# Order of the output projection, of the residual loads, and of the last chunked heads in a two-layer mixer kernel

## The chip, the cores and the metric

The kernel runs on one core of one Trainium2 chip. The metric is the device time of one execution in microseconds (us). Three runs of the kernel before gave 1920.71, 1923.3 and 1924.99 us, so its median is 1923.3 us. Times "at 382.7" are microseconds from the start of the profiled execution's span.

## What is computed

Two layers (`DEPTH` = 2) over 512 rows of 1024 values in float32. Each layer multiplies its input with a wide matrix `w_in`, runs three attention branches on the slices, gates and sums them, and projects the sum with `w_out`; a residual and a normalisation follow, then a feed-forward block (FFN) with its own residual and normalisation.

```python
h = jnp.einsum('bsd,de->bse', x, w_in[l])
rq, rk, rv, rg, cq, ck, cv, dq, dk, dv, gates = jnp.split(h, splits, axis=-1)
o_a = _retention(...)          # 4 heads
o_b = _chunk_attention(...)    # 8 heads
o_c = _diff_attention(...)     # 4 heads, two score matrices each
g = jax.nn.sigmoid(gates + b_merge[l]).reshape(B, S, N_BRANCHES, D)
merged = (g[:, :, 0] * (o_a @ w_branch_a[l]) + g[:, :, 1] * (o_b @ w_branch_b[l])
          + g[:, :, 2] * (o_c @ w_branch_c[l]))
mix = jnp.einsum('bsd,de->bse', merged, w_out[l])
x = _layer_norm(DEEPNORM_ALPHA * x + mix, ln1_g[l], ln1_b[l])
u_gate, u_up = jnp.split(jnp.einsum('bsd,df->bsf', x, w_ffn_in[l]), 2, axis=-1)
ffn = jnp.einsum('bsf,fd->bsd', jax.nn.silu(u_gate) * u_up, w_ffn_out[l])
x = _layer_norm(DEEPNORM_ALPHA * x + ffn, ln2_g[l], ln2_b[l])
```

## The kernel before

Every float32 operand is split into a high and a low part (`xTh`, `xTl`; `wh`, `wl`), and a product is three matmuls (`mm3`, lines 122 to 124). The high part is a cast on ACT, the low part a subtraction on DVE that needs the cast. The program is a list of *items*. An item names its weights and a function with two products, j = 0 and j = 1; between the two, and behind the second, small *groups* of other work are called (`between`). Weights are fetched up to three items ahead: the DMA into a staging tile `st` (4 of them), the cast to `wh` on ACT and the subtraction to `wl` on DVE (3 of each).

**What sets the order on the engines.** The code is traced once and a scheduler lays it out: each engine runs its queue strictly in the laid order and waits at the head of it. The scheduler takes work by program order where it is ready by its own estimate. One rule of it matters here: almost all tiles come from one pool `g` of 61 slots, and all matmul outputs from one pool of 8 PSUM banks, and in each pool the instructions that write a tile for the first time are laid out in program order, over all engines. A first writer that is late holds back the first writers of all tiles that the code makes after it. A bank goes to the next tile when the tile that had it has been read for the last time.

**The last chunked heads.** For head h, `s_c1(h)` makes four score products (`psc`, 4 banks) and the softmax (DVE line 437, ACT line 439), `s_c2(h)` transposes them (`ptr`, 10 transposes, 3 banks) and splits them into `cPh` and `cPl` (line 106, 112), and `s_c3(h)` multiplies with the values (`pco`, 1 bank; the copy `cos` on ACT, line 941, then the sum `cot` on DVE, line 942, which frees the bank). `u_dqk(h)` projects the queries and keys of differential head h (`pt`, 24 matmuls each) and rotates them: four copies `sw` on ACT, three DVE operations that make `rot`, and casts to `qs` or `ks` on ACT. `s_d0(0, 0)` makes the first score products of the differential heads, `v_back(dv)` reloads eight value tiles, `u_gate(1, i)` computes gates.

```python
(u_dqk(0), *c(7)), (u_gate(1, 0), *c(8)), (u_dqk(1), [v_back(dv)], [s_c3(7)] + d(0)[1]), (u_branch(1, 0), *d(1)),
```

`c(7)` stands for the groups `[s_c3(5), s_c1(7)]` and `[s_c2(6)]`, `c(8)` for `[s_c3(6)]` and `[s_c2(7)]`; `d(0)[1]` is `[s_d0(0, 0)]`.

**Branch C and the merge.** `u_branch(2, i)` multiplies the differential output (`oc`, made by `s_d4`) with `w_branch_c` into columns i and i + 4, multiplies with the gate (line 1083), adds to the sum of the other branches (`acc`, line 1087) and splits the result: `m` (of i) and `m2` (of i + 4). `s_mleft(k)` and `s_mright(k)` make the differences `sa` and `sb` of columns k and k + 4 and split them into `s12` and `s43`.

**The output projection** is a scheme of seven products in place of eight (`Chain`): `m1`, `m2`, `y`, `x`, `v`, `g`, `h`, 24 matmuls each. `m1` uses `m`, `m2` and `h` use `m2`, `y` and `x` use `s12`, `v` and `g` use `s43`. Its weights are sums of quarters of `w_out`: one staging tile is loaded for `m1`, and after the split for `m1` a DMA on the POOL queue adds the next quarter to it (line 178) for `y`, then in the same way for `x`, then for `h`. `m2` and `v` have plain loads, `g` a tile of its own (`c`). The results are added to the residual rows `z` (8 tiles; `load_res`, lines 459 and 1175 to 1178), whose last addition is followed by the statistics and, in the item with `whole`, by the normalisation; `bc` are four tiles of the norm's factors (line 465). `s_turned(0)` transposes the normalised rows 0 to 255 (`px`) for the FFN.

Of the kernel before, what the change touches and what calls it, by code (L numbers as in the profile page):

```python
# [15 lines left out]
ALU = mybir.AluOpType  # L16

P = 128
S = 512
D = 1024  # L20
NT = S // P
# [35 lines left out]
def trunk(ctx, tc, x_in, xT_in, w_in, ret_norm_g, da_norm_g, lq1, lk1, lq2, lk2, w_a, w_b, w_c, b_merge, w_out,  # L57
# [558 lines left out]
    def layer(l):  # L616
# [253 lines left out]
        def v_back(dst):  # L870
            def fn():
                for k, away in list(dst.items()):
                    dst[k] = g(F32R, "vhl")
                    nc.sync.dma_start(f(dst[k]), away)
            return fn
# [48 lines left out]
        def s_c3(h):  # L924
            def fn():
                p, j = divmod(h, 2)
                if j == 0:
                    ob[p] = g(name="cot")
                o_ = ob[p]
                pT = cP.pop(h)  # L930
                ps = bank("pco")
                for mt in range(NT):
                    b, o = PACK[mt]
                    w = S - P * mt
                    vt, c = v_of(cv, mt, h, 64)
                    hi = (ps[:, P * mt:], vt[:, c:c + P], pT[b].hi[:, o:o + w])
                    lo = (ps[:64, P * mt:], vt[:, c:c + 64], pT[b].lo[:, o:o + w])
                    for x in ((hi, lo) if mt == 0 else (lo, hi)):
                        nc.tensor.matmul(*x, start=mt == 0 and x is hi, stop=mt == NT - 1 and x is hi)
                t = g(name="cos")  # L940
                nc.scalar.copy(t[:64], ps[64:128])
                nc.vector.tensor_add(o_[64 * j:64 * j + 64], ps[:64], t[:64])
                if j:
                    ob[p] = Pair("ob")
                    split(ob[p], o_)
            return fn
# [5 lines left out]
        def u_dqk(h):  # L952
            def fn(wt):
                if "cd" not in tabs:
                    tabs["cd"], tabs["sd"], tabs["mask"] = g(name="cosd"), g(name="sind"), g(name="mask")
                    nc.sync.dma_start(tabs["cd"], rope_da[0])
                    nc.sync.dma_start(tabs["sd"], rope_da[1])
                    nc.vector.memset(tabs["mask"], 0.0)
                    nc.vector.memset(tabs["mask"][0:64, 0:64], -NEG)
                dqk[h] = QK()  # L960
                dqk[h].set_q(rotary(proj_T(xT, wt, 0), tabs["cd"], tabs["sd"], 32), -DA_DH ** -0.5)
                between()
                dqk[h].set_k(rotary(proj_T(xT, wt, P), tabs["cd"], tabs["sd"], 32))
            return [([wcols(DQ + P * h, P), wcols(DK + P * h, P)], KT)], fn
# [99 lines left out]
        def u_gate(br, i):  # L1064
            def fn(wt):
                for j, d in enumerate(tiles(br, i)):
                    gate_done(br, d, proj_T(xT, wt, P * j), (br, i) in EARLY)
                    between()
            return [(cols_of(W, GATE + D * br, br, i), KT)], fn
# [31 lines left out]
        def s_mleft(k):  # L1101
            def fn():
                mq[k].left(acc[k], acc[k + 4], 0.5)
            return fn
# [6 lines left out]
        def c(i):  # L1111

            return ([st(h) for st, h in ((s_c3, i - 2), (s_c1, i)) if 0 <= h < CA_HEADS],
                    [s_c2(i - 1)] if 0 <= i - 1 < CA_HEADS else [])

        def d(i):
# [6 lines left out]
                mid = [s_d3(h - 1)] if h >= 1 else []  # L1123
            return mid, [s_d0(h, j)]

        def u_rvg(hp):
            return u_two(Close(W, 0, 4, (RV + 512 * hp, RG + 512 * hp)), xq,
                         functools.partial(rv_done, hp), functools.partial(rg_done, hp))
# [11 lines left out]
        for (specs, fn), *groups in start + [  # L1140
            (w["x"], [p["a"]]), (u_gate(0, 3),), (w["g"],), (w["h"], [p["c"]]),
            (p["m1"], [s_dh(0)]), (p["y"], [], [s_r1(0)]), (p["v"], [s_dh(1)]), (p["m2"], [], [s_r1(1)]),
            (p["x"], [q["a"]]), (u_rqk(rq, RQ, 1),), (p["g"], [q["c"]]), (p["h"],),
            (q["m1"], [], [s_r2(0)]), (q["y"], [s_r2(1)]), (u_rqk(rk, RK, 1), [], [s_r3(0)]),
            (q["v"], [s_dh(2)], [s_r3(1)]), (q["m2"], [], [s_r1(2)]), (q["x"], [s_dh(3)]), (u_cqk(0), [], [s_r1(3)]), (q["g"],), (q["h"],),
            (u_gate(2, 0), [s_r2(2)], [s_r2(3), s_r3(2)]), (u_cqk(1), [s_r3(3)] + c(0)[0], c(0)[1]),
            (u_branch(0, 0), c(1)[0] + [v_back(cv)], c(1)[1]), (u_branch(0, 1), *c(2)), (u_cqk(2), *c(3)),
            (u_branch(0, 2), *c(4)), (u_cqk(3), *c(5)), (u_branch(0, 3), *c(6)), 
            (u_dqk(0), *c(7)), (u_gate(1, 0), *c(8)), (u_dqk(1), [v_back(dv)], [s_c3(7)] + d(0)[1]), (u_branch(1, 0), *d(1)),
            (u_gate(1, 1), [], d(2)[0] + d(2)[1]), (u_branch(1, 1), *d(3)), (u_dqk(2),),  # L1150
            (u_gate(1, 2), *d(4)), (u_branch(1, 2), *d(5)), (u_dqk(3),),
            (u_gate(1, 3), *d(6)), (u_branch(1, 3), *d(7)), (u_gate(2, 1), [s_d4(2)], [s_d2(3)]),
            (u_gate(2, 2), [s_d3(3)], [s_d4(3)]),
            (u_branch(2, 0), [], [s_mleft(0)]), (u_branch(2, 1), [], [s_mleft(1)]), (u_gate(2, 3), [s_mright(0)], [s_mright(1)]),
            (u_branch(2, 2), [], [s_mleft(2)]), (u_branch(2, 3), [], [s_mleft(3)]),
        ]:
            item(specs, fn, *groups)


        x1 = {}  # L1160
        x1T = [None] * KT
        x1f, x1q = {}, {}

        def load_res(x, src):
            x["z"] = [[g(name="z") for _ in range(2)] for _ in range(NT)]
            x["fresh"] = {(t, hf) for t in range(NT) for hf in range(2)}
            for t in range(NT):
                load_rows(x["z"][t], src[P * t:P * t + P])

        def plus(x, t, hf, ps, op, final=False):  # L1170

            z = x["z"][t][hf]
            if (t, hf) in x["fresh"]:
                x["fresh"].remove((t, hf))
                nc.vector.scalar_tensor_tensor(z, z, ALPHA, ps, op0=ALU.mult, op1=op)
            else:
                nc.vector.tensor_tensor(z, z, ps, op=op)  # L1177
            if final:
                x["n"].stats(t, hf)

        def out_items():

            hv = Chain(w_out[l], 0, 4)
            w = {}

            def it(name, i, hf, op, last=False, whole=False):
                def fn(wt):
                    if name == "m1":
                        load_res(x1, x_in if l == 0 else saved[2 * l - 1])
                        x1["n"] = Norm(x1["z"], v["g1"], v["b1"], bcast_rows(ln1_g[l:l + 1]), bcast_rows(ln1_b[l:l + 1]),  # L1190
                                       x1T, saved[2 * l], x1f)
                    on = {"x": "m1", "g": "m1", "h": "m1", "v": "y"}.get(name, name)
                    for j in range(2):
                        t = 2 * i + j
                        w[on, j] = product(mq, name, j, wt, w.pop((on, j), None))
                        plus(x1, t, hf, w[on, j], op, last)
                        if name in ("m2", "v", "h"):
                            w.pop((on, j))
                        if whole:
                            x1["n"].normalise(t)  # L1200
                        between()
                return [getattr(hv, name)], fn

            add, sub = ALU.add, ALU.subtract
            return {"c": hv.ahead_c, "m1": it("m1", 0, 0, add), "m2": it("m2", 0, 0, add, True), "y": it("y", 1, 1, add),
                    "x": it("x", 0, 1, sub), "v": it("v", 0, 1, add, True, True), "g": it("g", 1, 1, sub, True),
                    "h": it("h", 1, 0, add, True, True)}

        def s_turned(hf):
            def fn():  # L1210
                for b in range(4):
                    x1["n"].transposes_of(hf, b)
                if hf == 0:
                    x1q.update({i: Quarters(x1T[i], x1T[i + 4]) for i in range(4)})
            return fn

        o = out_items()
        for (specs, fn), *groups in [
            (o["m1"], [s_mright(2)], [o["c"]]), (o["m2"], [s_mright(3)]), (o["y"],), (o["x"],), (o["v"],),
            (o["g"], [], [s_turned(0)]), (o["h"],),  # L1220
        ]:
            item(specs, fn, *groups)

        hid = [None] * FT

# [233 lines left out]
```

## Time and profile before

| quantity | value |
|---|---|
| median of 3 runs | 1923.3 us |
| profiled execution, its own time | 1925.2 us |
| its span | 1923.4 us |
| ACT and DVE busy | 990.2 and 1391.6 us |
| mean granted clock of TensorE | 0.99 |

The profile's page has one row per engine with its busy time and a row of clock tenths. A view of waits lists, for one engine, who waited for whom (engine, line and tile of the waiting instruction, then of the releaser; total, times, longest). A view of windows has one row for a stretch A:B: its length, then for each engine the busy time and the number of instructions, the granted clock of TensorE, the share of the DMA engines and GB/s. A timeline has start, duration, engine, line, operation, output <- inputs, shapes, count, and in brackets the idle time before it with its releaser.

### The profile page before, as it was taken

To read this page: it belongs to the slowest core of one execution; us is meant where nothing else is said; L and a number is where in the kernel's file an instruction comes from. 1 tells how busy PE (TensorE), PEld (TensorE's weight loads), DVE (VectorE), ACT (ScalarE), POOL (GpSimd) and SP (SyncE) were. 2 spreads that over 40 slices of the span, in tenths; PEclk is the share of its full clock that TensorE was granted. 3 is DMA by queue.
4 is the path that set the end of the run, shared out by engine and by line. 5 is a ranking of instruction groups with operands and counts; after the bars stand their busy time and mean duration, and the time that the engine had idled before them with its cause. 6 is when DMAs were issued, how large, how long until landed. Compare 5 with 4: busy or idle time off the path is not lost. (4 is left out here: it accounts for less than half of the span.)

```text
span 1923.4 us, 23342 instructions
## 1 busy us (share of the span) xinstructions
PE 1874.9 (97%) x8754; PEld 1553.5 (81%) x8754; DVE 1391.6 (72%) x2117; ACT 990.2 (51%) x1593; POOL 132.6 (7%) x153
## 2 busy tenths in 40 slices
PE   9999999899998999999999999998999989999998
PEld 7788888778876788888878888887788768888886
DVE  6777756757677777789586768566675777778886
ACT  5555645656643544555264555456565445455541
POOL 2000000000001000010020000000000010000100
PEclk9999999999999999999999999999999999999999
DMA  9584453232267666788476844532322765777871
GB/s 289 170 269 132 121 170 116 87 99 66 82 176 175 158 175 186 181 231 197 147 221 192 247 110 142 179 90 83 110 66 72 210 161 160 184 188 206 210 197 44
DMA packets 235938, 302.89 MB, mean 157 GB/s; under 512 B 8757, under 2 KB 127633, under 8 KB 235825
## 3 DMA queue, kind: packets, MB, share of 16 engines
q1 hardware_dynamic: 205488, 242.25, 38.7%
q0 software_dynamic: 30336, 59.15, 17.7%
q8 instruction: 69, 1.13, 0.2%
q14 instruction: 45, 0.36, 0.1%
HBM read 279.29 MB, written 22.07 MB: 157 GB/s over the span
## 5 line engine op out<-in xcount | busy, mean ns | idle before, releaser
L272 DVE TENSOR_TENSOR wl<-st,wh 128x2048 fp32r<-128x2048 f32 x140 | 320.3, 2290 | 134.9 <-ACT wh L271 134.2
L271 ACT CAST wh<-st 128x2048 fp32r<-128x2048 f32 x140 | 267.3, 1914 | 249.6 <-PE pf L124 115.5
L122 PE MATMUL pt<-xTh,wh 128*128 128x512 f32 x960 | 378.7, 395 | 2.2 <-ACT wh L154 1.8
L124 PE MATMUL pt<-xTh,wl 128*128 128x512 f32 x960 | 375.3, 391 | 0.0
L123 PE MATMUL pt<-xTl,wh 128*128 128x512 f32 x960 | 375.2, 391 | 0.0
L155 DVE TENSOR_TENSOR wl<-st,wh 128x1024 fp32r<-128x1024 f32 (+1 forms) x188 | 200.8, 1085 | 69.1 <-ACT wh L154 46.8
L154 ACT CAST wh<-st 128x1024 fp32r<-128x1024 f32 (+1 forms) x188 | 173.5, 944 | 118.4 <-PE pt L123 44.5
L122 PEld LDWEIGHTS pt<-xTh,wh 128*128 128x128 f32 x960 | 181.4, 189 | 40.6 <-ACT wh L154 2.9
L124 PEld LDWEIGHTS pt<-xTh,wl 128*128 128x128 f32 x960 | 180.9, 188 | 38.2
L123 PEld LDWEIGHTS pt<-xTl,wh 128*128 128x128 f32 x960 | 181.0, 189 | 36.8 <-DVE xTl L112 0.2
L122 PE MATMUL pf<-wh,xTh 128*128 128x512 f32 x336 | 133.6, 398 | 2.3 <-ACT rph L106 0.9
L123 PE MATMUL pf<-wl,xTh 128*128 128x512 f32 x336 | 131.1, 390 | 0.0
L124 PE MATMUL pf<-wh,xTl 128*128 128x512 f32 x336 | 130.3, 392 | 0.0
L122 PE MATMUL pf<-wh,s43h 128*128 128x512 f32 x256 | 101.3, 396 | 6.4 <-ACT s43h L108 6.4
L122 PE MATMUL pf<-wh,s12h 128*128 128x512 f32 x256 | 101.5, 397 | 3.2 <-ACT wh L271 3.2
L123 PE MATMUL pf<-wl,s12h 128*128 128x512 f32 x256 | 101.0, 395 | 3.6 <-DVE wl L272 3.6
L123 PE MATMUL pf<-wl,s43h 128*128 128x512 f32 x256 | 100.9, 394 | 0.0
L124 PE MATMUL pf<-wh,s12l 128*128 128x512 f32 x256 | 100.7, 394 | 0.0
L124 PE MATMUL pf<-wh,s43l 128*128 128x512 f32 x256 | 100.3, 393 | 0.0
L746 ACT COPY tc<-pf 128x512 f32<-128x512 f32 x84 | 48.5, 590 | 81.2 <-PE pf L124 76.0
L122 PEld LDWEIGHTS pf<-wh,xTh 128*128 128x128 f32 x336 | 63.1, 188 | 19.8 <-ACT xTh L106 2.3
L124 PEld LDWEIGHTS pf<-wh,xTl 128*128 128x128 f32 x336 | 62.5, 188 | 15.3 <-DVE xTl L112 2.7
(327 smaller groups left out, 3681.5 us busy)
## 6 DMA issues: line engine op xcount, KB each, us to landing
st<-in_w_in SPq DMA_DIRECT2D x53, 1024.0 KB, 6.3
st<-in_w_ffn_in SPq DMA_DIRECT2D x38, 1024.0 KB, 5.9
st<-in_w_in SPq DMA_DIRECT2D x48, 512.0 KB, 5.2
st<-in_w_ffn_in POOLq DMA_DIRECT2D x20, 1024.0 KB, 10.8
st<-in_w_ffn_out SPq DMA_DIRECT2D x20, 1024.0 KB, 7.9
st<-in_w_ffn_out POOLq DMA_DIRECT2D x16, 1024.0 KB, 9.0
st<-in_w_in POOLq DMA_DIRECT2D x12, 1024.0 KB, 11.1
st<-in_w_ffn_in SPq DMA_DIRECT2D x24, 512.0 KB, 5.5
```

Source lines behind the costliest of these rows:

```text
L122: nc.tensor.matmul(ps, lh, rh, start=start, stop=False, skip_group_check=onto)
L123: nc.tensor.matmul(ps, lh, rl, start=False, stop=False, skip_group_check=onto)
L124: nc.tensor.matmul(ps, ll, rh, start=False, stop=stop, skip_group_check=onto)
L154: return [nc.scalar.copy(self.hi[:, a:b], self.st[:, a:b]), nc.vector.tensor_sub(self.lo[:, a:b], self.st[:, a:b], f(self.hi[:, a:b]))]
L155: nc.vector.tensor_sub(self.lo[:, a:b], self.st[:, a:b], f(self.hi[:, a:b]))]
L271: nc.scalar.copy(self.hi, st)
L272: nc.vector.tensor_sub(self.lo, st, f(self.hi))
L746: nc.scalar.copy(t[to, j], ps)
```

## The change

In both layers:

1. The output projection runs `m1, m2, y, v, x, g, h`. `x` now closes its rows (statistics and normalisation), no longer `v`.
2. The eight residual loads and the construction of the norm leave the function of `m1` and become the group `rows_in`, behind the second product of `u_gate(2, 2)` and ahead of `s_d4(3)`. The four loads of the norm's factors become the group `norm_rows` in `x`.
3. `s_mleft(2)` moves from behind `u_branch(2, 2)` to behind `u_branch(2, 3)`, ahead of `s_mleft(3)`. The load and the addition for `g` (`o["c"]`) move from `m1` to the first group of `u_branch(2, 2)`.
4. `s_c2(6)` moves from behind the key projection of `u_dqk(0)` to the group between its two projections, ahead of `s_c1(7)`.
5. `s_c3(7)` and `s_d0(0, 0)` move from behind the key projection of `u_dqk(1)` to the group between its two projections, behind `v_back(dv)`.

The other lines of the diff only move the functions ahead of their first use.

```diff
+        def rows_in():
+            load_res(x1, x_in if l == 0 else saved[2 * l - 1])
+            x1["n"] = Norm(x1["z"], v["g1"], v["b1"], None, None, x1T, saved[2 * l], x1f)
+
+        def norm_rows():
+            x1["n"].gam, x1["n"].bet = bcast_rows(ln1_g[l:l + 1]), bcast_rows(ln1_b[l:l + 1])
...
-                    if name == "m1":
-                        load_res(x1, x_in if l == 0 else saved[2 * l - 1])
-                        x1["n"] = Norm(x1["z"], v["g1"], v["b1"], bcast_rows(ln1_g[l:l + 1]), bcast_rows(ln1_b[l:l + 1]),
-                                       x1T, saved[2 * l], x1f)
...
-                    "x": it("x", 0, 1, sub), "v": it("v", 0, 1, add, True, True), "g": it("g", 1, 1, sub, True),
+                    "x": it("x", 0, 1, sub, True, True), "v": it("v", 0, 1, add), "g": it("g", 1, 1, sub, True),
...
-            (u_dqk(0), *c(7)), (u_gate(1, 0), *c(8)), (u_dqk(1), [v_back(dv)], [s_c3(7)] + d(0)[1]), (u_branch(1, 0), *d(1)),
+            (u_dqk(0), [s_c3(5), s_c2(6), s_c1(7)]), (u_gate(1, 0), [s_c3(6)], [s_c2(7)]),
+            (u_dqk(1), [v_back(dv), s_c3(7)] + d(0)[1]), (u_branch(1, 0), *d(1)),
...
-            (u_gate(2, 2), [s_d3(3)], [s_d4(3)]),
+            (u_gate(2, 2), [s_d3(3)], [rows_in, s_d4(3)]),
...
-            (u_branch(2, 2), [], [s_mleft(2)]), (u_branch(2, 3), [], [s_mleft(3)]),
+            (u_branch(2, 2), [o["c"]]), (u_branch(2, 3), [], [s_mleft(2), s_mleft(3)]),
...
-            (o["m1"], [s_mright(2)], [o["c"]]), (o["m2"], [s_mright(3)]), (o["y"],), (o["x"],), (o["v"],),
+            (o["m1"], [s_mright(2)]), (o["m2"], [s_mright(3)]), (o["y"],), (o["v"],), (o["x"], [norm_rows]),
             (o["g"], [], [s_turned(0)]), (o["h"],),
```

More of the change, by code (lines that the diff above doesn't have):

```diff
@@ L1124, in d, with load_res, plus @@
             return mid, [s_d0(h, j)]
+        x1 = {}
+        x1T = [None] * KT
+        x1f, x1q = {}, {}
+        def load_res(x, src):
+            x["z"] = [[g(name="z") for _ in range(2)] for _ in range(NT)]
+            x["fresh"] = {(t, hf) for t in range(NT) for hf in range(2)}
+            for t in range(NT):
+                load_rows(x["z"][t], src[P * t:P * t + P])
+        def plus(x, t, hf, ps, op, final=False):
+            z = x["z"][t][hf]
+            if (t, hf) in x["fresh"]:
+                x["fresh"].remove((t, hf))
+                nc.vector.scalar_tensor_tensor(z, z, ALPHA, ps, op0=ALU.mult, op1=op)
+            else:
+                nc.vector.tensor_tensor(z, z, ps, op=op)
+            if final:
+                x["n"].stats(t, hf)
@@ new lines, in rows_in, with out_items, it, fn @@
+        def rows_in():
[3 more added lines that the diff above has]
+            x1["n"].gam, x1["n"].bet = bcast_rows(ln1_g[l:l + 1]), bcast_rows(ln1_b[l:l + 1])
+        def out_items():
+            hv = Chain(w_out[l], 0, 4)
+            w = {}
+            def it(name, i, hf, op, last=False, whole=False):
+                def fn(wt):
+                    on = {"x": "m1", "g": "m1", "h": "m1", "v": "y"}.get(name, name)
+                    for j in range(2):
+                        t = 2 * i + j
+                        w[on, j] = product(mq, name, j, wt, w.pop((on, j), None))
+                        plus(x1, t, hf, w[on, j], op, last)
+                        if name in ("m2", "v", "h"):
+                            w.pop((on, j))
+                        if whole:
+                            x1["n"].normalise(t)
+                        between()
+                return [getattr(hv, name)], fn
+            add, sub = ALU.add, ALU.subtract
+            return {"c": hv.ahead_c, "m1": it("m1", 0, 0, add), "m2": it("m2", 0, 0, add, True), "y": it("y", 1, 1, add),
+                    "x": it("x", 0, 1, sub, True, True), "v": it("v", 0, 1, add), "g": it("g", 1, 1, sub, True),
+                    "h": it("h", 1, 0, add, True, True)}
@@ L1126, in u_rvg, with s_turned, fn @@
+        def s_turned(hf):
+            def fn():
+                for b in range(4):
+                    x1["n"].transposes_of(hf, b)
+                if hf == 0:
+                    x1q.update({i: Quarters(x1T[i], x1T[i + 4]) for i in range(4)})
+            return fn
+        o = out_items()
         def u_rvg(hp):
@@ L1152, in layer @@
             (u_gate(1, 3), *d(6)), (u_branch(1, 3), *d(7)), (u_gate(2, 1), [s_d4(2)], [s_d2(3)]),
-            (u_gate(2, 2), [s_d3(3)], [s_d4(3)]),
+            (u_gate(2, 2), [s_d3(3)], [rows_in, s_d4(3)]),
             (u_branch(2, 0), [], [s_mleft(0)]), (u_branch(2, 1), [], [s_mleft(1)]), (u_gate(2, 3), [s_mright(0)], [s_mright(1)]),
-            (u_branch(2, 2), [], [s_mleft(2)]), (u_branch(2, 3), [], [s_mleft(3)]),
[L1156 to L1187, printed above, removed]
-                    if name == "m1":
-                        load_res(x1, x_in if l == 0 else saved[2 * l - 1])
-                        x1["n"] = Norm(x1["z"], v["g1"], v["b1"], bcast_rows(ln1_g[l:l + 1]), bcast_rows(ln1_b[l:l + 1]),
-                                       x1T, saved[2 * l], x1f)
[L1192 to L1205, printed above, removed]
-                    "x": it("x", 0, 1, sub), "v": it("v", 0, 1, add, True, True), "g": it("g", 1, 1, sub, True),
-                    "h": it("h", 1, 0, add, True, True)}
@@ L1209, in s_turned @@
[L1209 to L1218, printed above, removed]
-            (o["m1"], [s_mright(2)], [o["c"]]), (o["m2"], [s_mright(3)]), (o["y"],), (o["x"],), (o["v"],),
+            (u_branch(2, 2), [o["c"]]), (u_branch(2, 3), [], [s_mleft(2), s_mleft(3)]),
```

## The prediction, on record before the result

> **What bounds the kernel now.** I read the page first, then the waits of PE, then windows around the two places that the diff touches, then the timelines of the engines there. The page says which engine is full:
>
> ```profile
> PE 1874.9 (97%) x8754; PEld 1553.5 (81%) x8754; DVE 1391.6 (72%) x2117; ACT 990.2 (51%) x1593; POOL 132.6 (7%) x153
> ```
>
> The change adds and removes no matmul, so it can only win back time in which PE stands still or runs at a reduced clock. The waits of PE name the places:
>
> ```profile
> PE pco L939 <- ACT cPh L106: 9.5, 2, 4.8
> PE pf L122 <- ACT s43h L108: 6.4, 2, 4.8
> PE psc L422 <- DVE cot L942: 5.4, 2, 2.7
> PE pf L122 <- ACT m L108: 3.8, 2, 1.9
> PE pf L123 <- DVE wl L272: 3.6, 2, 1.8
> PE pf L122 <- ACT wh L271: 3.2, 2, 2.3
> ```
>
> Each happens twice, once per layer, and all six lie in the code that the diff reorders: the first and third in the last chunked heads, the others in the output projection. What all of it costs is read from one window per stage and layer:
>
> ```profile
> 357.20:430.40 73.20, 65.29 (x291) 52.93 (x290) 43.01 (x87) 40.09 (x80) 1.04 (x2) 0.93 0.31 94
> 568.10:615.80 47.70, 38.37 (x146) 30.07 (x145) 31.79 (x44) 14.50 (x12) 3.68 (x4) 0.89 0.76 205
> 1315.20:1386.40 71.20, 63.44 (x287) 51.31 (x285) 43.00 (x87) 39.71 (x79) 1.04 (x2) 0.95 0.31 96
> 1524.50:1569.60 45.10, 36.37 (x146) 28.27 (x144) 31.55 (x45) 15.47 (x13) 3.06 (x3) 0.92 0.79 216
> ```
>
> Loss is the length less PE's busy time, plus the length times what the granted clock lacks to 1. Heads, layer 0: 73.20 − 65.29 = 7.91 idle and 0.07 × 73.2 = 5.1 of clock, 13.0 in all; layer 1: 7.76 + 3.56 = 11.3. Projection, layer 0: 9.33 + 5.25 = 14.6; layer 1: 8.73 + 3.61 = 12.3. The sum, **51.2 us**, bounds the gain: 1874 would be the floor.
>
> **The heads (points 4 and 5).** Why PE stood still:
>
> ```profile
> 365.24 0.44 PE L122 MATMUL pt<-xTh,wh 128*128 128x512 f32 x1
> 370.77 1.25 PE L452 MATMUL ptr<-ident,cE 128*128 128x128 f32 x10
> 382.72 0.80 PE L939 MATMUL pco<-cPh,vhl 128*128 128x512 f32 x1 [4.76 <-ACT cPh L106]
> 414.42 0.44 PE L422 MATMUL psc<-ks,qs 128*128 128x384 f32 x1 [2.69 <-DVE cot L942]
> ```
>
> ```profile
> 367.39 1.29 ACT L108 ACTIVATE qs<-rot 64x512 fp32r<-64x512 f32 x2 [2.08 <-DVE rot L391]
> 368.71 0.58 ACT L941 COPY cos<-pco 64x512 f32<-64x512 f32 x1
> 379.51 2.54 ACT L106 CAST ks<-rot 64x512 fp32r<-64x512 f32 x4 [1.98 <-DVE rot L391]
> 382.08 1.07 ACT L106 CAST cPh<-ptr 128x512 fp32r<-128x512 f32 x2
> ```
>
> The transposes of head 6 are done at 372.02, yet `cPh` is cast at 382.08, right behind the key casts. In the code `s_c2(6)` stands behind the key projection, so its first writers stand behind `ks` in pool order, and ACT waits 1.98 us for the rotation. With `s_c2(6)` ahead of the keys, `cPh` follows its transposes by a few us, long before PE reaches `s_c3(6)` at 378: the 4.76 goes.
>
> What is late next is a PSUM bank. Between the projections now stand, in order, `pco(5)`, three `ptr`, four `psc`, and then the key projection. With the query `pt` that is nine banks, the keys' is the tenth; two must have come free. The query's comes free early. The second is `pco(5)`'s, freed by `cot`:
>
> ```profile
> 369.50 0.68 DVE L942 TENSOR_TENSOR cot<-pco,cos 64x512 f32<-64x512 f32 x1
> 413.68 0.68 DVE L942 TENSOR_TENSOR cot<-pco,cos 64x512 f32<-64x512 f32 x1 [0.44 <-ACT cos L941]
> ```
>
> `cot` ends at 370.18, because `cos` (368.71) stands behind the `qs` casts, which wait for the rotation. Before, PE filled this time with the key projection (from 365.24). Now the transposes run in it, and it runs dry 1.25 us later than 365.24, at 366.5: **a new wait of 3.7**. Bounds: 0 if a bank comes free earlier; 5.6 if it is the first `ptr`, which is split on ACT behind `cos` and then on DVE, by my estimate at 372.1 (`cot`'s end, a cast of 1.07, a subtraction of some 0.7). I take 3.7, since that bank's own row shows the end.
>
> `s_c3(7)` and `s_d0(0, 0)` ahead of the keys of `u_dqk(1)`: the 2.69 is the same pattern (`cot` at 413.68 behind the key rotation), and it goes. Bounds: 0 to 2.7 of it stays, since the value reloads stand ahead of `cos(7)` in pool order:
>
> ```profile
> 397.37 8.78 SPq L874 DMA_DIRECT2D vhl<-v  x8
> ```
>
> They are issued by 406.2. PE reached the stall at 411.73; without the key product (24 matmuls of 0.23, 5.5) it has done `s_c3(7)` at 406.2 as well, so `cos(7)` hardly waits; I take 0. The keys of head 1 are rotated later by about the 3 us that the inserted work takes, and PE has work of `s_d0(0, 1)` and the gates beside it: 1.0 for a wait of the next transposes, bounds 0 and 3. Half clock: the rows of before show what a stall does to the clock.
>
> ```profile
> 1372.00:1375.40 3.40, 3.31 (x10) 2.42 (x9) 3.05 (x11) 2.31 (x9) 0.00 (x0) 0.50 0.02 5
> ```
>
> This window stands behind the layer-1 copy of the 2.69 stall: 3.4 us at half clock, 1.7 lost. So I put 1.7 behind the new 3.7, bounds 0 and 3.4.
>
> (The Trainium skill, page "TensorE: Matmul & The Clock Gate", section "What's actually happening", gives the half rate only after a whole idle window of about 3.4 us. This row speaks against that, since 2.69 was enough, and the measurement decides. By the rule the stalls forecast below 3.4 us would cost no clock, and the time would be an estimated 3.4 us less than mine.)
>
> New loss 3.7 + 1.0 + 1.7 = 6.4 per layer, so the heads gain 13.0 − 6.4 = **6.6** and 11.3 − 6.4 = **4.9**.
>
> **The projection (points 1 to 3).**
>
> ```profile
> 570.29 1.90 ACT L271 CAST wh<-st 128x2048 fp32r<-128x2048 f32 x1 [4.85 <-DMA st<-in_w_out]
> 572.63 0.40 ACT L108 ACTIVATE m<-th 128x256 fp32r<-128x256 f32 x1
> 587.30 5.52 ACT L271 CAST wh<-st 128x2048 fp32r<-128x2048 f32 x3 [8.65 <-DMA st<-in_w_out]
> 602.10 1.90 ACT L271 CAST wh<-st 128x2048 fp32r<-128x2048 f32 x1 [6.43 <-DMA st<-in_w_out]
> 603.91 0.63 ACT L108 ACTIVATE s43h<-sb 128x512 fp32r<-128x512 f32 x1
> 1557.60 1.91 ACT L271 CAST wh<-st 128x2048 fp32r<-128x2048 f32 x1 [5.62 <-DMA st<-in_w_out]
> ```
>
> ```profile
> 589.25 2.29 DVE L272 TENSOR_TENSOR wl<-st,wh 128x2048 fp32r<-128x2048 f32 x1 [6.99 <-ACT wh L271]
> 594.25 0.42 DVE L304 TENSOR_TENSOR sb<-th,sa 128x256 f32<-128x256 f32 x1
> ```
>
> ```profile
> 561.78 1.28 POOL L178 DMA_DIRECT2D st<-in_w_out  x1 [11.03 <-DVE wl L272]
> 591.83 1.28 POOL L178 DMA_DIRECT2D st<-in_w_out  x1 [13.43 <-DVE wl L272]
> ```
>
> *v ahead of x.* `x`'s weights are the second accumulation: cast at 587.30, `wl` ready at 591.54, and PE waits for both (2.7 us in layer 0, 4.1 in layer 1). `v` has plainly loaded weights and 5.5 us of matmuls (24 of 0.23: 142 take 32.11 in the window further down), which cover that. This wait goes.
>
> *`s43h` (4.75 and 1.6).* `sb` of columns 2 starts only at 594.25, because in pool order it follows the residual tiles, which are first written by the first of these loads (the second row is the branches' own, with the time to landing):
>
> ```profile
> 568.06 5.46 SPq L459 DMA_DIRECT2D z<-in_x  x8
> th<-th SPq DMA_DIRECT2D x40, 256.0 KB, 4.5
> ```
>
> Then `s43h` of column 3 (603.91) stands behind the cast at 602.10, which waits for a DMA. With the loads made earlier and `norm_rows` later, `sb` follows `m` directly, some 20 us before `v`. But `v` now comes one product (5.5 us) sooner; I leave 0.5, bounds 0 and 3.
>
> *Residual loads.* `rows_in` puts eight tiles ahead of `och(3)`, the last operand of branch C, and eight loads ahead of `u_branch(2, 0)`'s own load on SP. The z row prices the issue: 5.46, eight of 0.68.
>
> ```profile
> 539.10 0.68 DVE L1083 SCALAR_TENSOR_TENSOR th<-th,pt 128x512 f32<-128x512 f32 x1
> 539.10:571.50 32.40, 32.11 (x142) 26.27 (x140) 25.62 (x42) 13.41 (x19) 2.61 (x2) 1.00 0.77 193
> ```
>
> PE goes on with `u_branch(2, 1)` and `u_gate(2, 3)` where only the last k is missing, so PE hides it; without that cover it would be a stall of 5.5. The merge on DVE begins 5.1 later (539.10 to 544.2). It has 32.40 − 25.62 = 6.8 of idle time to catch up in, and the three operations of `s_mleft(2)` are out of its way.
>
> *m of column 3 (1.87).* The last addition before its cast began at 569.36 and ended at 570.05, and the cast ran at 572.63, behind the weight cast of `y` and `s12h`:
>
> ```profile
> 569.36 0.68 DVE L1087 TENSOR_TENSOR th<-th 128x512 f32<-128x512 f32 x1
> 573.08 0.66 PE L122 MATMUL pf<-wh,m 128*128 128x512 f32 x1 [1.87 <-ACT m L108]
> ```
>
> `s12h` is now behind it, which alone leaves 1.87 − 0.52 = 1.35. If no idle time of DVE is used up, the addition ends at 570.05 + 5.1 and `m` at 575.6, against PE at 571.2: 4.35. I take the middle, **2.8**.
>
> *h.* The third accumulation hangs on `x`'s low part (591.54), which nothing here moves: DMA at 591.83, cast at 602.10, 1.90, then 2.29 for `wl`: 606.3. PE gets to `h` at 568.1 + 6 products of 5.52 (33.1) + 2.8 + 0.5 + 1.7 = 606.2. Wait 0.2, bounds 0 and 3. In layer 1, 1557.60 + 1.91 + 2.29 = 1561.8 against 1524.5 + 33.1 + 5.0 = 1562.6: 0. Point 3's load for `g` starts earlier and lies beside matmuls; cost 0, and without that cover the 1.28 of its issue. Half clock behind the 2.8: 1.7, bounds 0 and 3.4.
>
> New loss 2.8 + 0.5 + 0.2 + 1.7 = 5.2 and 5.0, so the projection gains 14.6 − 5.2 = **9.4** and 12.3 − 5.0 = **7.3**.
>
> **The sum.** 6.6 + 4.9 + 9.4 + 7.3 = 28.2 from the profiled execution's 1925.2: **1897.0 us**. That execution is 1.9 above the median of 1923.3; its span is 1923.4, with 1.8 around it.
>
> **The rivals.**
>
> 1. *The bank is there.* If `cos` gets ahead of `qs` or a `psc` bank is found, the 3.7 and its 1.7 fall away in both layers: 1897.0 − 10.8 = 1886. For it: ACT is idle from 365.31 to 367.39, and `cos`'s input is ready by then. Against it: `cos` also stood behind `qs` in the trace of before. Chance 0.13.
>
> 2. *The stalls move.* The bank comes from a `ptr` (5.6, with 3.4 of clock), the reloads hold back `cos(7)` so that 2.7 stays, and `v`, called 5.5 us earlier, waits 3 for `s43`. Per layer 1.9 + 1.7 + 2.7 + 2.5 = 8.8 less gain, less the 1.0 on `d2`: 1897.0 + 15.6 = 1912.6. For it: pool order decided all six waits of before. Chance 0.17.
>
> 3. *It doesn't do what it says*: the layout already used the idle time as well as the pools allow, and the losses come back elsewhere: 1921 to 1927. Against it: each wait has its own releaser, and these are taken out. Chance 0.05.
>
> 4. *Slower: the residual tiles find no room.* If fewer than 8 of pool `g`'s 61 slots are free at 535, some of the eight loads wait for slots of the input's tiles, which are read until the last gate product:
>
> ```profile
> 557.00 0.39 PE L124 MATMUL pt<-xTh,wl 128*128 128x512 f32 x1
> ```
>
> SP issues in order, so the branch's own load waits behind them: about 557.4 + 5.5 + 4.5 to land = 567, in place of 539 for the first merge step. PE meanwhile does the branch products and stops before `m1`, since the merge needs about 20 of the 25.6 us of DVE in the window above: `m1` starts at about 587 in place of 568, 19 us, and 1 to 2 of clock. Twice that on 1897 gives 1937. Against it: I count some 34 live tiles there, 42 with the eight. It decides when my count is off by 20. Chance 0.13, which also has to hold other ways of being slower.
>
> **How the numbers follow.** Main case 0.52. A difference of 0.2% (3.8 us) is about what a measurement of this kernel can tell. Faster: 0.52 + 0.13 + 0.17 = 0.82; same 0.05; slower 0.13. The main case alone, its bounds added as independent, reaches 1888 to 1907; with rivals 1 and 2 and their own spread the range is 1883 to 1918, and rivals 3 and 4 lie outside it.
>
> **What would show it.** Right: PE waits near 366.5 for 3 to 4 us, before the first key `pt`, released by `cot` L942; no wait of `pco` for `cPh` and none of `psc` for `cot`; `v` starts with no wait for weights; `sb` directly behind `m`; `z` loads near 530 on SP; the heads' windows 5 to 7 us shorter, the projection's 7 to 9. Wrong: a wait of more than 5 us before `m1`, the branch products pausing for `och`, SP waiting in the `z` loads, or `h` waiting for its weights for more than 3 us.

## The result and the profile after

| kernel | median, us | runs | ratio to before (95% interval) |
|---|---|---|---|
| before | 1924.2 | 13 | |
| changed | 1918.0 | 13 | 0.997 (0.9961 to 0.9978) |

The change makes the kernel 6.2 us faster, 0.3%, where 1897.0 was forecast. The profiled execution of the changed kernel has a span of 1917.2 us. Its row of engines on the page:

```profile
PE 1868.9 (97%) x8754; PEld 1553.1 (81%) x8754; DVE 1390.2 (73%) x2117; ACT 989.9 (52%) x1593; POOL 136.5 (7%) x153
```

The waits of PE in the changed kernel (who waited, for whom, total, times, longest):

```profile
PE pf L122 <- ACT m L108: 13.4, 2, 6.7
PE pt L122 <- DVE cot L942: 7.4, 2, 3.7
PE pf L123 <- DVE wl L272: 4.3, 3, 1.9
PE ptr L452 <- DVE dE L985: 2.8, 2, 1.4
PE pf L122 <- DVE rs L497: 2.1, 2, 1.2
PE pf L122 <- ACT s12h L108: 1.7, 2, 0.9
```

The waits of `pco` for `cPh` (9.5 before), of `psc` for `cot` (5.4) and of `pf` for `s43h` (6.4) are gone. The wait for a PSUM bank came at 3.70 us, as forecast to the second digit. But the wait for `m`, 3.8 before and forecast to grow to 5.6, is now 13.4.

The windows of the two stages, as before: length, busy time of PE first, granted clock behind POOL.

```profile
356.70:425.20 68.50, 63.26 (x298) 52.10 (x297) 43.64 (x88) 42.23 (x82) 1.04 (x2) 0.97 0.33 100
562.90:612.50 49.60, 37.77 (x149) 29.03 (x149) 39.22 (x55) 18.58 (x17) 6.48 (x4) 0.90 0.72 170
1309.50:1377.00 67.50, 62.26 (x294) 51.41 (x293) 42.89 (x88) 42.22 (x82) 1.04 (x2) 0.97 0.33 102
1515.50:1564.50 49.00, 37.58 (x149) 28.86 (x147) 39.19 (x55) 18.57 (x17) 6.48 (x4) 0.90 0.71 172
```

The heads lose less (5.2 us idle at a clock of 0.97), the projection loses more than before: 11.8 idle and 5.0 of clock in layer 0, 11.4 and 4.9 in layer 1. Since the work in the windows is not cut at the same matmul, the better account is by the start of the same matmul in both traces:

| first matmul of | before, us | changed, us | lead | gained since the row above |
|---|---|---|---|---|
| `u_dqk(0)`, layer 0 | 357.20 | 356.75 | 0.45 | |
| `m1`, layer 0 | 568.11 | 562.96 | 5.15 | 4.7: the heads |
| `u_dqk(0)`, layer 1 | 1315.18 | 1309.54 | 5.64 | 0.5: projection and FFN |
| `m1`, layer 1 | 1524.49 | 1515.49 | 9.00 | 3.4: the heads |
| end of the span | 1923.4 | 1917.2 | 6.2 | −2.8: projection and FFN |

So the heads brought 8.1 of the forecast 11.5 us, and the projection lost 2.3 where 16.7 had been forecast. What stands ahead of the wait for `m`? First PE and ACT of the changed kernel (timelines: start, duration, engine, line, operation, and in brackets the idle time and its releaser):

```profile
562.96 0.39 PE L122 MATMUL pf<-wh,m 128*128 128x512 f32 x1
572.02 0.80 PE L122 MATMUL pf<-wh,m 128*128 128x512 f32 x1 [6.62 <-ACT m L108]
```

```profile
569.75 1.90 ACT L271 CAST wh<-st 128x2048 fp32r<-128x2048 f32 x1 [3.20 <-DMA st<-in_w_out]
571.55 0.41 ACT L108 ACTIVATE m<-th 128x256 fp32r<-128x256 f32 x1
571.87 0.61 ACT L108 ACTIVATE m2h<-th 128x512 fp32r<-128x512 f32 x1
573.06 0.42 ACT L108 ACTIVATE m<-th 128x256 fp32r<-128x256 f32 x1 [0.58 <-DVE th L1087]
```

The cast of `m` stands behind the weight cast of `y`, and that waits for the accumulating DMA. The DMA was issued at 561.24, for it needs `wl` of `m1`, and this stands on DVE among the merge. The merge was late because of one row, the fourth product of line 1083 in DVE's order (the first ran at 539.99); it is the second product of `u_branch(2, 0)`:

```profile
541.79 1.28 DVE L1083 SCALAR_TENSOR_TENSOR th<-th,pt 128x512 f32<-128x512 f32 x2
551.72 0.69 DVE L1083 SCALAR_TENSOR_TENSOR th<-th,pt 128x512 f32<-128x512 f32 x1 [5.90 <-DMA th<-th]
```

DVE stood 5.90 us for a gate tile, the *second* of the two that `u_branch(2, 0)` loads. The queue of SP in the changed kernel and in the kernel before:

```profile
518.89 4.88 SPq L459 DMA_DIRECT2D z<-in_x  x8
524.24 0.33 SPq L1081 DMA_DIRECT2D th<-th  x1
533.72 7.96 SPq L174 DMA_DIRECT2D st<-in_w_out  x2
541.77 1.13 SPq L1081 DMA_DIRECT2D th<-th  x1
```

```profile
523.39 0.37 SPq L174 DMA_DIRECT2D st<-in_w_out  x1
523.80 0.51 SPq L1081 DMA_DIRECT2D th<-th  x1
539.21 0.37 SPq L174 DMA_DIRECT2D st<-in_w_out  x1
539.62 0.50 SPq L1081 DMA_DIRECT2D th<-th  x1
```

The first gate tile is issued at the same time in both. The second stood behind one weight load, and now stands behind two; the second of the two waits at the head of the queue for a staging tile, so that it starts 7.6 us after the first (533.72 and 541.30). The gate tile is issued 2.2 us later, while everything around it runs 5 us earlier, and from its issue to its use on DVE pass another 9.95 us.

### The profile page after: what moved, and what is told of

The parts are those of the page before. It is cut to its first block, busy times and chain, and to the rows that moved or that the text cites. A ratio compares the mean times of both kernels' runs of the same rounds, so it can differ in the third digit from the quotient of the medians.

```text
span 1917.2 us, 23308 instructions
## 1 busy us (share of the span) xinstructions
PE 1868.9 (97%) x8754; PEld 1553.1 (81%) x8754; DVE 1390.2 (73%) x2117; ACT 989.9 (52%) x1593; POOL 136.5 (7%) x153
## 3 DMA queue, kind: packets, MB, share of 16 engines
q1 hardware_dynamic: 205488, 242.25, 38.4%
## 5 line engine op out<-in xcount | busy, mean ns | idle before, releaser
L124 PEld LDWEIGHTS pt<-xTh,wl 128*128 128x128 f32 x960 | 180.9, 188 | 38.4
L123 PEld LDWEIGHTS pf<-wl,xTh 128*128 128x128 f32 x336 | 63.1, 188 | 13.5 <-DVE wl L272 1.3
```

The costliest lines, as they stand in the source:

```text
L123: nc.tensor.matmul(ps, lh, rl, start=False, stop=False, skip_group_check=onto)
L124: nc.tensor.matmul(ps, ll, rh, start=False, stop=stop, skip_group_check=onto)
```

## The experiments

All times are medians of 4 to 11 executions, each ratio against runs of the kernel before on the same chip (medians 1924.0 to 1924.6). The ratio is the safer number: where the executions of a run differ by some us, as in run 1, the median can be off by one or two.

| run | kernel | median, us | ratio (95% interval) |
|---|---|---|---|
| 1 | heads alone | 1914.65 | 0.9959 (0.9945 to 0.9972) |
| 2 | changed, load for `g` back in `m1` | 1908.73 | 0.9923 (0.9910 to 0.9937) |
| 3 | changed, residual rows late | 1912.20 | 0.9942 (0.9929 to 0.9954) |
| 4 | changed, gate tiles first | 1903.64 | 0.9896 (0.9883 to 0.9910) |
| 5 | changed, `x` ahead of `v` | 1920.25 | 0.9979 (0.9970 to 0.9987) |
| 6 | changed, `s_mleft(2)` back | 1920.80 | 0.9979 (0.9970 to 0.9988) |
| 7 | changed, `s_c1(7)` behind the keys | 1907.72 | 0.9915 (0.9901 to 0.9928) |
| 8 | 4 and 2 together | 1907.83 | 0.9915 (0.9901 to 0.9928) |
| 9 | 4 and 7 together | 1894.47 | 0.9850 (0.9835 to 0.9865) |
| 10 | 9 with `s_mleft(2)` back | 1896.31 | 0.9859 (0.9845 to 0.9874) |
| 11 | 9 with `s_d0(0, 0)` behind the keys | 1905.05 | 0.9900 (0.9884 to 0.9917) |
| 12 | projection alone | 1926.49 | 1.0009 (1.0000 to 1.0018) |

### Each half alone: runs 1 and 12

Run 1 is the kernel before with points 4 and 5:

```diff
-            (u_dqk(0), *c(7)), (u_gate(1, 0), *c(8)), (u_dqk(1), [v_back(dv)], [s_c3(7)] + d(0)[1]),
+            (u_dqk(0), [s_c3(5), s_c2(6), s_c1(7)]), (u_gate(1, 0), [s_c3(6)], [s_c2(7)]),
+            (u_dqk(1), [v_back(dv), s_c3(7)] + d(0)[1]),
```

> Points 4 and 5 alone (the chunked heads and d0), the rest as before. The landmarks of the two traces put the gain of this part at 4.7 us in layer 0 and 3.4 in layer 1. If that reading is right: 1924 - 8 = 1916 us, with the 3.70 wait on cot L942 and no cPh wait, and the projection's waits as before. If instead the output projection brought the gain of the whole change and the heads nothing: 1922 to 1926.

Run 12 is the changed kernel with the same lines the other way round.

> Points 1 to 3 alone (the order of the output projection, the early residual loads, the moved differences), the heads as before. If the parts add, the whole change less the first run leaves 1918.0 - 1914.65 = 3 us more than the kernel before: 1925 to 1929 us, with a wait for m of 6 to 7 us per layer. By the prediction this part alone gains 16.7: 1908 us.

By the medians the heads alone gain 9.7 us (1924.32 to 1914.65) and the projection alone loses 2.5 (1923.97 to 1926.49; the interval begins at 1.0000). By the ratios it is a gain of 7.9 (0.0041 of 1924) and a loss of 1.7, together 6.2, where the whole change gains 5.8 by its ratio and 6.2 by its medians: the parts add. Run 12 came in the first of its two ranges, far from the 1908 of the prediction. Its waits begin thus:

```profile
PE pf L122 <- ACT m L108: 13.6, 2, 6.9
PE pco L939 <- ACT cPh L106: 9.4, 2, 4.7
PE psc L422 <- DVE cot L942: 5.3, 2, 2.7
```

The long wait for `m` is a matter of points 1 to 3 alone, and needs no earlier end of the heads.

### What makes the second gate tile late: runs 2, 3, 4 and 8

Run 2 moves the load for `g` back, run 3 the residual rows, run 4 takes neither away but issues the two gate tiles first:

```diff
-            (u_branch(2, 2), [o["c"]]),
+            (u_branch(2, 2),),
...
-            (o["m1"], [s_mright(2)]),
+            (o["m1"], [s_mright(2)], [o["c"]]),
```

> The changed kernel with the load and addition for g back in m1's group. Theory A (the eight residual tiles ahead in pool order hold back the second gate tile load of the first branch C item, and with it the merge): nothing changes, the wait of pf for m stays at 6 to 7 us per layer, 1916 to 1920 us. Theory B (the staging load for g, moved ahead, holds that load back on SP): the second th load is issued some 8 us earlier, the wait for m falls to 2 or 3 us, about 1904 us.

```diff
-            (u_gate(2, 2), [s_d3(3)], [rows_in, s_d4(3)]),
+            (u_gate(2, 2), [s_d3(3)], [s_d4(3)]),
...
-            [s_mleft(2), s_mleft(3)]),
+            [s_mleft(2), s_mleft(3), rows_in]),
```

> The changed kernel with rows_in behind the last branch, as late as before. Theory A: th loads of the first branch C item go out before 540, the wait for m falls from 6.6 to about 2 us; but sb is again behind the residual loads, and v comes a product sooner, so s43h is waited for by 4 to 8 us; 1912 to 1920 us, the place of the wait being the test. Theory B: the wait for m stays at 6 to 7 us.

```diff
+        def th_in():
+            for d in tiles(2, 0):
+                away, th[2, d] = th[2, d], g(name="th")
+                nc.sync.dma_start(th[2, d], away)
...
-                    if (br, i) in EARLY:
+                    if (br, i) in EARLY and br == 0:
...
-            (u_gate(2, 2), [s_d3(3)], [rows_in, s_d4(3)]),
+            (u_gate(2, 2), [s_d3(3)], [th_in, rows_in, s_d4(3)]),
```

> The changed kernel with both gate tile loads of the first branch C item issued at the head of rows_in's group, ahead of the residual loads (and not in the item). Theory A: the 5.9 us of idle DVE ahead of the third product of the merge go, the wait for m falls from 6.6 to 1 to 3 us per layer with a half clock window less, 1903 to 1910 us. Theory B, or a merge that is held by something else (the weight casts of y, which wait for the accumulating DMA): the wait for m stays above 5 us, 1916 to 1920 us.

Run 4 gains 14.4 us on the changed kernel. Its merge on DVE, then ACT and PE at `m1`:

```profile
538.55 1.29 DVE L1083 SCALAR_TENSOR_TENSOR th<-th,pt 128x512 f32<-128x512 f32 x2 [5.69 <-PE pt L124]
```

```profile
564.40 1.90 ACT L271 CAST wh<-st 128x2048 fp32r<-128x2048 f32 x1 [4.87 <-DMA st<-in_w_out]
566.20 0.41 ACT L108 ACTIVATE m<-th 128x256 fp32r<-128x256 f32 x1
566.67 0.50 PE L122 MATMUL pf<-wh,m 128*128 128x512 f32 x1 [1.40 <-ACT m L108]
```

The first two products of line 1083 now run as a pair, DVE waits for PE and no longer for a DMA, and the weight cast of `y` comes 5.35 us earlier. The wait for `m` is 1.40, close to the 1.35 that the prediction had as its lower bound. So the late arrival of the second gate tile was the cause of the long wait.

What put it there? With the rows late (run 3) SP issues it at 534.71, behind one weight load:

```profile
534.30 0.37 SPq L174 DMA_DIRECT2D st<-in_w_out  x1
534.71 0.50 SPq L1081 DMA_DIRECT2D th<-th  x1
```

With the load for `g` late (run 2) it keeps its place behind two, and is issued at 541.88:

```profile
541.88 0.46 SPq L1081 DMA_DIRECT2D th<-th  x1
```

That is theory A's order, yet run 2 gained 9.3 us, where theory A expected none and theory B 14. DVE had the tile earlier:

```profile
547.68 0.69 DVE L1083 SCALAR_TENSOR_TENSOR th<-th,pt 128x512 f32<-128x512 f32 x1 [1.76 <-DMA th<-th]
```

From issue to use it took 5.8 us, against 9.95 in the changed kernel (541.77 to 551.72). The one thing moved is the load and addition for `g`: in the changed kernel its accumulating DMA is issued on POOL at 539.45, two microseconds ahead of the gate tile, in run 2 at 547.65. So both moves delayed this load: the residual rows its issue, the addition for `g` its landing. It took both to make the loss: PE waits 2.42 for `m` in run 2, at most 2.2 in run 3, and 6.62 in the changed kernel. That the addition slows the other transfer by sharing the DMA engines is the reading of these two traces; nothing measured it alone.

> Both gate tile loads first (as in the fourth run) and the load and addition for g back in m1's group. If that addition cost only by slowing the landing of the second th load (10 us in the changed kernel, 6 without it), there is nothing left of it here: 1902 to 1905 us, like the fourth run. If it holds back the weights or the merge by itself as well: 1896 to 1900 us.

Run 8 was expected at 1905 or below and came at 1907.83, 4.2 us slower than run 4 (3.7 by the ratios, whose intervals just overlap, though each of its four executions is slower than each of run 4's) and only 0.9 faster than run 2. So with `g` late the place of the gate tiles is worth 0.9 us, and with `g` early 14.4. Once the gate tiles are safe, the early place for `g` seems the better one. Late, its addition is issued shortly ahead of the one for `y` (POOL, the first two rows), and the cast for `y` on ACT waits longer:

```profile
548.98 1.33 POOL L178 DMA_DIRECT2D st<-in_w_out  x1 [23.34 <-DVE sa L294]
555.27 1.28 POOL L178 DMA_DIRECT2D st<-in_w_out  x1 [4.95 <-DVE wl L272]
565.40 1.90 ACT L271 CAST wh<-st 128x2048 fp32r<-128x2048 f32 x1 [6.09 <-DMA st<-in_w_out]
```

From the issue for `y` to its cast it takes 10.1 us (555.27 to 565.40), in run 4 8.9 (555.48 to 564.40), and PE waits 2.61 for `m` in place of 1.40. That the addition for `g` is what slows the one for `y` is again a reading of the traces.

Run 3 at 1912.20 was in its range, and the wait for `m` fell to about 2 us as expected (3.9 in both layers). But the rest of the time was not lost where it was put: no wait for `s43h` of 4 us came. Its residual rows are issued only at 575.70, and PE waits for the additions to `z`, which read its banks:

```profile
575.70 7.07 SPq L459 DMA_DIRECT2D z<-in_x  x8
PE pf L122 <- DVE z L1141: 4.8, 4, 2.1
```

With the rows early in run 4 these waits are gone: early rows are worth 8.6 us (1912.20 to 1903.64), but only behind the gate tiles; ahead of them they cost 5.8 (1918.0 to 1912.20).

### `v` ahead of `x`, and `s_mleft(2)`: runs 5, 6 and 10

```diff
-            "x": it("x", 0, 1, sub, True, True), "v": it("v", 0, 1, add),
+            "x": it("x", 0, 1, sub), "v": it("v", 0, 1, add, True, True),
...
-            (o["y"],), (o["v"],), (o["x"], [norm_rows]),
+            (o["y"],), (o["x"], [norm_rows]), (o["v"],),
```

> The changed kernel with x ahead of v again (x without, v with statistics and normalisation), all else as changed. In the changed kernel's trace PE still starts x ahead of v: 11 of its 24 matmuls stand before v's, and the waits of 0.9 and 1.85 us are there. If so, the swap in the program bought little: 1916 to 1922 us. By the prediction's step (v covers x's weights, 2.7 and 4.1 us) undoing it costs that: about 1925 us.

1920.25 is in the first range: undoing the swap costs 2.3 us by the medians, less than the 6.8 of the prediction's step, and the intervals of the two ratios overlap, so it is not clear that it costs anything. The order of PE in the changed kernel, counted from its queue between `m2` and `h`:

```
before:   y 24, x 24, v 24, g 24
changed:  y 24, x 11, v 24, x 13, g 24
```

The swap in the program is half a swap on PE. `x`'s and `v`'s products add to banks that `m1` and `y` opened, so bank order doesn't bind them; that this is why the scheduler laid out 11 of `x`'s matmuls first is a reading, not a test. They wait as `x` did before (1.85 for `wl`, against 1.82).

Run 5 shows more. With `x` ahead of `v` in the program, `x`'s low part is made 2.3 us earlier on DVE (from 588.06, against 590.37 in the changed kernel), and PE does not wait for `x`'s weights at all: there is no row for `wl` or `wh` of the projection in its waits. In its place `h` waits for the norm, up to 4.47 us:

```profile
PE pf L122 <- DVE rs L497: 7.3, 2, 4.5
```

The rows of the two views of waits add up to the same (38.4 us, and 38.5 in the changed kernel). What run 5 has beside them is a stretch of 6.8 us at about half clock behind the 4.47, some 3.4 us by estimate. So whatever the swap is worth, it is not that `v` covers `x`'s weights: it puts several short waits in the place of a long one for the norm.

```diff
-            (u_branch(2, 2), [o["c"]]), (u_branch(2, 3), [], [s_mleft(2), s_mleft(3)]),
+            (u_branch(2, 2), [o["c"]], [s_mleft(2)]), (u_branch(2, 3), [], [s_mleft(3)]),
```

> The changed kernel with s_mleft(2) back behind u_branch(2, 2). By the prediction's step (its operations out of the merge's way) the wait of pf for m grows by 1 to 2 us per layer: 1920 to 1923 us. Rival: y's wait for s12h of column 3 (0.9 us) shrinks instead, since the differences start earlier, and m waits for the weight cast of y anyway: 1915 to 1918 us.

> As the ninth run, with s_mleft(2) back behind u_branch(2, 2). y's wait of some 4 us for s12h of column 3 goes, as it did in the sixth run; if x's weights then set the time anyway, it comes back as a wait for wl of 2 to 4 us and the total stays at 1891 to 1896 us; if s12h itself was the bound, 1886 to 1889 us.

1920.80 and 1896.31, 2.8 and 1.8 us slower than without this edit, but in both cases the intervals of the ratios overlap, so neither loss is clear of noise. Run 6 lies in the range of the prediction's step by luck: the wait for `m`, which should have grown, stays (13.6 in all), and the wait for `x`'s low part grows from 4.3 to 8.0:

```profile
PE pf L122 <- ACT m L108: 13.6, 2, 6.9
PE pf L123 <- DVE wl L272: 8.0, 2, 4.0
```

With the differences late, part of `y` waits for `s12h` and lets `x`'s weights come meanwhile; with them early, `x`'s weights themselves are the bound. The rows of the two views of waits add up to nearly the same (38.7 us in run 6, 38.5 in the changed kernel). Run 10's total came in the first of its two ranges, with the wait for `wl` that this range named (4.0 per layer).

### The bank: runs 7, 9 and 11

```diff
-            (u_dqk(0), [s_c3(5), s_c2(6), s_c1(7)]),
+            (u_dqk(0), [s_c3(5), s_c2(6)], [s_c1(7)]),
```

> The changed kernel with s_c1(7) behind the key projection of u_dqk(0), s_c2(6) still ahead of it. If the 3.70 us wait is the tenth PSUM bank, it goes (the keys' tile is then the sixth), and 3.4 us at half clock per layer with it: 1918 - 2 x (3.7 + 1.7) = 1907 us. Rival: the wait moves to the scores or transposes of head 7, which now come later: 1914 us or more, with a new wait of 2 us or more before 400.

1907.72: a gain of 10.3 us, 0.7 from the first expectation. In the heads' window of run 7 PE is busy for 61.49 of 63.30 us at full clock:

```profile
356.70:420.00 63.30, 61.49 (x300) 50.81 (x298) 43.49 (x88) 42.34 (x83) 1.04 (x2) 1.00 0.35 109
```

So the 3.70 is the bank: four score banks fewer ahead of the keys, and no wait of more than 0.3 us takes its place there (`pt` for `cPl`).

> The changed kernel with both repairs: the gate tile loads first, and s_c1(7) behind the keys. If the two losses are independent, their gains add: 1903.6 - 10.3 = 1893 us (1891 to 1896), near the 1897 that was forecast for the change itself. If the first repair only moved a wait that the second opens again: above 1898.

1894.47, within the spread of the sum (1903.64 − 10.3 = 1893.3): the two gains add. This version is the fastest of all, 29.7 us ahead of the kernel before on its chip (1924.17). The first row is its longest remaining wait in the projection, and `s12h` of column 3 stands on ACT behind a weight cast (that of `x`, 576.24), which waits 6.57 us for its DMA:

```profile
PE pf L122 <- ACT s12h L108: 7.6, 2, 3.9
PE ptr L452 <- DVE dE L985: 2.8, 2, 1.4
576.24 1.90 ACT L271 CAST wh<-st 128x2048 fp32r<-128x2048 f32 x1 [6.57 <-DMA st<-in_w_out]
578.04 0.62 ACT L108 ACTIVATE s12h<-sa 128x512 fp32r<-128x512 f32 x1
```

```diff
-            (u_dqk(1), [v_back(dv), s_c3(7)] + d(0)[1]),
+            (u_dqk(1), [v_back(dv), s_c3(7)], d(0)[1]),
```

> As the ninth run, with s_d0(0, 0) behind the keys of u_dqk(1) again and s_c3(7) still ahead of them. The 1.38 us wait of the transposes for dE should go if the longer chain behind the keys was its cause, or grow by the time that d0 is later: 1890 us or 1896 us and more. By the prediction's step the 2.69 wait for cot stays away, since s_c3(7) is still ahead.

1905.05. The wait for `dE` went, as the first half of the expectation has it, and no wait for `cot` came back; but a bank wait of 5.11 came in the gates after the second group of scores, in both layers, which the expectation does not name:

```profile
411.20 0.79 PE L122 MATMUL pt<-xTh,wh 128*128 128x512 f32 x1 [5.11 <-DVE mx L437]
```

Two sets of four scores with one branch item between them leave no bank, and the next product waits for line 437 to read one. So `s_d0(0, 0)` ahead of the keys, the second half of point 5, is worth 10.6 us here, or 5.3 per layer. The prediction had credited both halves of point 5 together with 2.69 per layer.

## Why the prediction was wrong

**The direction was right, the size was not**: 28.2 us forecast, 6.2 measured; and the measured 1918.0 lies at the very end of its range.

**The heads, 11.5 forecast, 8.1 read from the traces and 7.9 by the ratio of run 1: right in the mechanism, too small in one term.** The 4.76 and the 2.69 went, the bank wait came at 3.70 from the `cot` that was named (and run 7 shows that it is the bank), the transposes waited 1.38 where 1.0 was put. Mis-sized was the clock: it was put at one half-clock window of 1.7 per layer, and in the profiled execution there are two in each, in layer 0 behind the 3.70 and from 424.5, behind the 1.38. The two windows more are 3.4 us, about the difference of 11.5 and 8.1.

**"Residual loads": the step that failed.** It put the eight loads down as 5.46 us of issue on SP, let the merge begin 5.1 later (how the one gives the other is not said), and let it catch up in DVE's idle time. The merge's first product did come later, at 539.99 against 534.19 in run 3, which has the rows late. But that was not the issue on SP: the eight loads went out from 518.89 in 4.88 us, not near 530, and the first gate tile at 524.24, some 15 us before its use. What holds this first product is not shown. It did no harm: in run 4 it still runs only at 538.55. PE ran through the branch products without a pause (busy for 35.19 of the 35.20 us from 530.2 to 565.4), and pool `g` had room, so rival 4 did not occur. What the step missed is that it counted `u_branch(2, 0)`'s *one* load, where the item makes two. The second gate tile was pushed not by the length of eight loads but behind another weight load, which holds the queue until a staging tile is free, here for 7.6 us. Run 3 shows that the early rows do it, and run 4 that with the tiles safe the wait for `m` is 1.40 and not 6.62. That pool order is what puts the tile behind the weight load is the reading by the scheduler's rule.

**Point 3, "cost 0".** This is the second half of the same failure. It was called hidden beside matmuls. The addition for `g` lies beside matmuls, but also beside that gate tile load, and run 2 is 9.3 us faster without it there. In run 8 the same move costs 4.2. It has no price by itself; it depends on what it runs beside.

***m* of column 3, 2.8.** The lower bound of 1.35 was the mechanism of run 4 (behind the weight cast of `y`); the upper bound of 4.35 was passed, since the step held the weight cast of `y` fixed at 570.29. It moves with the merge, because the DMA that it waits for needs `wl` of `m1`, which is made on DVE among the merge.

***v* ahead of *x*, "this wait goes".** Wrong: 1.85 of it is still there, with the program swapped and PE's order only in part. And `v` is not what would take it away: with `x` ahead again (run 5) PE does not wait for `x`'s weights at all. Undoing the swap costs some 2.3, not clear of noise, against 6.8 forecast.

***s43h*, *h*, and a wait that the sum does not have.** `v` did not wait for `s43h`; 0.5 was forecast. `g` waited 1.25 and 0.85 for the norm's `rs`, and `h` 0.83 for its `mv` (line 495), not for weights; for `h` 0 to 0.2 was forecast. `y` waits for `s12h` of column 3: 0.93 and 0.82 in the changed kernel, and up to 3.9 in run 4, once the wait for `m` is short. The sum has no term for it, and it is the longest wait of the projection in run 4 (7.5 in both layers), which still lies 6.6 us above the forecast 1897.0.

Had the gate tiles gone first, the time would have been 1903.64, and with the bank also mended 1894.47. That this is near the forecast 1897.0 confirms nothing: this version lacks the 3.70 that the forecast counted, and has the `s12h` wait that the forecast did not count.

## What to carry to other kernels

A load that is moved ahead has a price for each load that follows in its queue and its pool, and the dear ones are those that a stalled load then separates from their use: list *every* transfer of the items behind it, not only the next. Where a queue is in order and its loads wait for free buffers, a place lost is worth the wait of the load in front (7.6 us here), not its issue time (0.4). And check the order on the engine, not in the program: swapping two items moved only 13 of 24 matmuls here.

## What the runs showed of the hardware

A stall of 1.38 us was enough for a half-clock window, and not always. In the changed kernel it is followed by one, in run 4 the same stall (1.38, ahead of 422.99) is not. First the changed kernel, the 3.4 us ahead and the window, then the same for run 4:

```profile
421.00:424.40 3.40, 1.86 (x10) 0.98 (x9) 2.55 (x9) 3.21 (x7) 0.00 (x0) 1.00 0.23 72
424.50:427.90 3.40, 3.40 (x14) 3.15 (x13) 3.10 (x5) 1.35 (x3) 0.00 (x0) 0.50 0.00 0
```

```profile
421.00:424.40 3.40, 1.86 (x10) 1.02 (x9) 2.42 (x8) 3.33 (x7) 0.00 (x0) 1.00 0.23 73
424.50:427.90 3.40, 3.40 (x21) 2.92 (x20) 3.35 (x8) 1.35 (x3) 0.00 (x0) 1.00 0.00 0
```

14 matmuls in one window, 21 in the other, though PE was busy for 1.86 of the 3.40 us ahead in both. Around the 6.62 us of the changed kernel's wait for `m` the stretch is 10.2 us long:

```profile
567.80:578.00 10.20, 5.98 (x14) 4.73 (x15) 8.09 (x13) 3.78 (x5) 0.70 (x1) 0.50 0.43 128
```

The Trainium skill, page "TensorE: Matmul & The Clock Gate", section "What's actually happening", has the clock judged in windows of about 3.4 us that run free of the kernel. The lengths of these stretches, 3.4 and three times that, agree; that a window must be idle throughout does not, since 1.38 us of idle sufficed. The same stall can thus cost 1.4 us or, by an estimate from the 7 matmuls of 0.23 that are missing, some 3 us. What decides between the two is not shown; where the stall falls against such windows may do it, and no run here tests that.
